# Smaller first loads, and x turned behind the products ahead of it, in a decoder-trunk step

## The chip, the cores and the metric

The kernel runs on one core of a Trainium2 chip. A core has TensorE (matrix products, PE in the profile, with PEld for its weight loads), VectorE (DVE), ScalarE (ACT), GpSimd (POOL) and SyncE (SP, which here issues most of the loads), and 16 DMA engines that move data between the chip's memory and the on-chip buffer. TensorE writes to PSUM, which the other engines read. Each engine works through its own instruction queue in order and waits on semaphores for the others.

The metric is the device time of one execution in microseconds (us); less is better. Where several executions were timed, the median is given.

## The reference

The reference computes one inference step of a decoder layer for 256 prompt tokens and 8 x 4 sample tokens, 288 tokens in all, with a model width of 2048, in float32:

```python
def rmsnorm(x, w):
    xf = x.astype(jnp.float32)
    y = xf * lax.rsqrt(jnp.mean(xf * xf, axis=-1, keepdims=True) + EPS)
    return (y * w.astype(jnp.float32)).astype(x.dtype)

def swiglu(x, w_in, w_out):
    gate, up = jnp.split(x @ w_in, 2, axis=-1)
    return (jax.nn.silu(gate) * up) @ w_out
...
        x = x + 0.5 * rmsnorm(swiglu(rmsnorm(x, g[0]), ffn1_w_in[l], ffn1_w_out[l]), g[1])
        m, sg, sh = hybrid_mixer(rmsnorm(x, g[2]), mix_w_in[l], gla_w_gate_up[l], gla_b_gate[l],
                                 gla_norm[l], lbs[l], hgrn_norm[l], mix_w_out[l], s_gla[l], s_hgrn[l])
        x = x + rmsnorm(m, g[3])
        x = x + 0.5 * rmsnorm(swiglu(rmsnorm(x, g[4]), ffn2_w_in[l], ffn2_w_out[l]), g[5])
```

There is one layer. The hidden width of each feed-forward part is 5632. The hybrid mixer runs two gated linear recurrences beside each other; the change does not touch it. The weights, some 365 MB, are read once.

## The kernel before

**Layout.** Activations lie turned: model width on the 128 partitions, tokens along the free axis. x is 16 tiles `x[k]` of 128 x 288 (256 prompt columns and 32 sample columns). Each product x @ w is taken with a weight tile of 128 x 128 as the stationary operand and a tile of 288 tokens as the moving one, and summed over the 16 values of k in PSUM.

**Three products for one.** Float32 operands are split into a high and a low part in the fast float32 format: `xh` and `xl` for activations (`split_to`, L241 to L244: ScalarE writes the high part, scaled by the norm's gain, and VectorE the low part), `wh` and `wl` for weights (`Weights.pieces`, L75 to L88: ScalarE copies, L86, and VectorE subtracts, L87). TensorE then takes `xh` with `wh`, `xl` with `wh`, and `xh` with `wl` (L464 to L466). The norm's per-token factor `rt` is not needed ahead of the products; it is multiplied in afterwards.

**Weights.** They come in units of 512 KB (two k rows of 512 columns) through `raw` buffers, of which there are three (`RAW_BUFS`). `load` (L55) issues one load on SyncE's queue; `fill` keeps three units loaded beyond the last one split; `ahead` splits units in advance, as many as the four `wh`/`wl` buffers hold. A `raw` buffer is free for the next load once its unit has been split.

**Blocks.** `block` (L455) runs the products of 512 output columns: for each unit of two k, four column groups f of three products, then a `tick(k)`, in which other work is put between products. The last unit runs column group by column group, and `evac` then moves the finished column group out of PSUM. The first two blocks of the kernel are `gate1_0` and `up1_0` in `ffn` (L499); in the first, `tick0` of `PreNorm` (L364) prepares a tile of x each k, and in the second, `tick1` sums the squares of x for the norm (`acc`, then `pre` and `rt` at k = 9). The gate tiles `g` are copied out of PSUM at L523 and get `rt` later.

**The start.** The norm gains go to `stage` over ScalarE's queue, are turned by TensorE (`tp_prm`, L269) and copied to `prm` (L270). x is loaded in four pieces of 512 columns (`xin`, L260 to L267), each as a prompt load of 512 KB and a sample load of 64 KB, with one weight unit behind each of the first three. `x_tile` (L272) turns one tile: three transposes into PSUM (L276, L277), a copy to `x[k]` by VectorE for even k (L281) and by ScalarE for odd k (L279), and the split into `xh` and `xl` from that copy. Four tiles are prepared ahead of the first product (`AHEAD`), with the first two units split in halves between them, each part pinned behind the one ahead of it (`issue_after`); the other twelve follow one for each `tick0`, four tiles ahead of use.

**Order.** A scheduler orders each engine's instructions by priority and estimated readiness; `issue_after` puts instructions behind a given one.

Of the kernel before, what the change touches and what calls it, by code (L numbers as in the profile page):

```python
# [23 lines left out]
KT = D // P  # L24
# [7 lines left out]
RAW_BUFS = 3  # L32
# [5 lines left out]
class Weights:  # L38
# [16 lines left out]
    def load(self):  # L55
        i, src = self.loaded, self.srcs[self.loaded]
        raw = self.rawp.tile([P, 1024], F32, name=f"raw{i}", tag="raw")
        if isinstance(src, list):
            for c, part in src:
                w = part.shape[2]  # L60
                self.nc.sync.dma_start(raw.rearrange("p (a b) -> p a b", b=512)[:, :, c:c + w], part)
        else:
            self.nc.sync.dma_start(raw.rearrange("p (a b) -> p a b", b=src.shape[2]), src)
        self.raws[i] = raw
        self.loaded += 1

    def fill(self):
        while self.loaded < min(len(self.srcs), self.split + RAW_BUFS):
# [2 lines left out]
    def part(self):  # L71
        for _ in self.pieces(1):
            pass
# [42 lines left out]
def trunk_kernel(ctx, tc, x_prompt, x_sample, state_gla, state_hgrn, norm_gains, f1_in, f1_out, f2_in, f2_out,  # L116
                 mix_in, gla_up, gla_b, gla_norm, hgrn_gamma, hgrn_norm, mix_out, masks,
                 y_prompt, y_sample, sgp, shp, sgs, shs):
    nc = tc.nc
    V, S, G, PE = nc.vector, nc.scalar, nc.gpsimd, nc.tensor  # L120
# [103 lines left out]
    lb = const.tile([P, 8], F32, name="lb")  # L224
    omlb = const.tile([P, 8], F32, name="omlb")

    AHEAD = 4
    UPDATED = 8
    EARLY = 4
# [8 lines left out]
    def gain(i, k):  # L238
        return prm[:, i * KT + k:i * KT + k + 1]

    def split_to(parts, src, col):  # L241
        i1 = S.activation(parts[0], src, AF.Copy, scale=col).ins
        i2 = V.scalar_tensor_tensor(parts[1], src, col, parts[0].bitcast(F32), op0=ALU.mult, op1=ALU.subtract).ins  # L243
# [6 lines left out]
    ldp = first.enter_context(tc.tile_pool(name="ld", bufs=4, side="right"))  # L250
# [6 lines left out]
    G.dma_start(stage2[12:14, :], gla_norm.rearrange("o (k p) -> (o k) p", p=P))  # L257
    G.dma_start(stage2[14:15, :], hgrn_norm)
    xins = []
    for s in range(4):  # L260
        xin = ldp.tile([P, 3, 512], F32, name=f"xin{s}", tag="xin")
        V.memset(xin[:, 2, :], 0.0)
        nc.sync.dma_start(xin[:, 0:2, :], x_prompt[0, :, s * 512:(s + 1) * 512].rearrange("(t p) c -> p t c", p=P))
        nc.sync.dma_start(xin[0:TS, 2, :], x_sample[:, :, s * 512:(s + 1) * 512].rearrange("b t c -> (b t) c"))
        xins.append(xin)
        if s < RAW_BUFS:
            W.load()  # L267
    tp = auxtile("tp_prm")
    PE.transpose(tp[:, 0:96], stage, ident[0:96, 0:96])  # L269
    V.tensor_copy(prm[:, 0:96], tp[:, 0:96])  # L270

    def x_tile(k):  # L272
        s, c = k // 4, slice(k % 4 * P, (k % 4 + 1) * P)
        tp = auxtile(f"tp_x{k}")
        for t in range(2):
            PE.transpose(tp[:, t * P:(t + 1) * P], xins[s][:, t, c], ident)  # L276
        PE.transpose(tp[:, TP:TP + P], xins[s][:, 2, c], ident)  # L277
        if k % 2:
            S.activation(x[k], tp[:, 0:T], AF.Copy)  # L279
        else:  # L280
            V.tensor_copy(x[k], tp[:, 0:T])  # L281
        return split_x(0, k)


    pin = ()
    for k in range(AHEAD):
        if k % 2 == 0:
            unit = W.pieces(2)
        for part in (lambda: x_tile(k), lambda: next(unit)):
            with ExitStack() as es:  # L290
                for i in pin:
                    es.enter_context(tc.issue_after(i))
                pin = part()
        if k % 2 == 1:
            W.fill()

    def prm2():
        tp = auxtile("tp_prm2")
        PE.transpose(tp[:, 0:P], stage2, ident)
        V.tensor_copy(prm[:, 96:111], tp[:, 0:15])  # L300


    V.tensor_scalar(hg1[:, 0:KT], prm[:, 16:32], 0.5, None, op0=ALU.mult)
    V.tensor_scalar(hg1[:, KT:], prm[:, 80:96], 0.5, None, op0=ALU.mult)

    def lower_bounds():

# [49 lines left out]
    class PreNorm:  # L357
# [4 lines left out]
            self.name, self.update, self.ahead, self.late = name, update, ahead, []  # L362

        def tick0(self, k):  # L364
            if k + self.ahead < KT:
                self.split = self.update(k + self.ahead)

        def tick1(self, k):
            if k < 8:
# [82 lines left out]
        return update  # L452


    def block(name, nk, rhs, evac, width=512, tick=None, tail=1, hold=False, most=99, fill=None):  # L455

        nf, per = width // P, 1024 // width
        nu = nk // per
        ps = [mmtile(f"{name}_{f}") for f in range(nf)]
        ws = [W.next() for _ in range(EARLY // per)] if fill else []  # L460

        def mm3(dst, w, f, k, parts, start, stop):
            c = (k % per) * width + f * P
            yield lambda: PE.matmul(dst, w[0][:, c:c + P], parts[0], start=start, stop=False)  # L464
            yield lambda: PE.matmul(dst, w[0][:, c:c + P], parts[1], start=False, stop=False)  # L465
            yield lambda: PE.matmul(dst, w[1][:, c:c + P], parts[0], start=False, stop=stop)  # L466

        def mm(w, f, k):
            if not fill or f or k >= EARLY:
                for ready in mm3(ps[f][:, 0:T], w, f, k, rhs(k), k == 0, k == nk - 1):  # L470
                    ready()

        if fill:
            fill.products(lambda dst, k, parts, stop: mm3(dst, ws[k // per], 0, k, parts, k == 0, stop), ps[0][:, 0:T])
        for u in range(nu - tail):
            w = ws.pop(0) if ws else W.next()
            for k in range(u * per, (u + 1) * per):
                for f in range(nf):
                    mm(w, f, k)
                if tick is not None:  # L480
                    tick(k)
            W.ahead(most)
            if fill and u == 5:
                fill.scaled()
        ws = [W.next() for _ in range(tail)]
        for f in range(nf):
            for k in range((nu - tail) * per, nk):
                mm(ws[k // per - (nu - tail)], f, k)
            evac(f, fill.total(ps[f][:, 0:T]) if fill and f == 0 else ps[f][:, 0:T])
        for k in range((nu - tail) * per, nk):  # L490
            if tick is not None:
                tick(k)
        if not hold:
            W.ahead()
# [4 lines left out]
    def ffn(tag, gcol, gnext, pn, before, fill=None):  # L499

        final = gnext is None
        border = []
        with ExitStack() as pools:
# [3 lines left out]
            def do_in(c):  # L507
                hh = fp.tile([P, 4, T], F32R, name=f"hh{tag}_{c}", tag="hh")
                hl = fp.tile([P, 4, T], F32R, name=f"hl{tag}_{c}", tag="hl")
                hid[c] = (hh, hl)  # L510
                gs = []

                def gate(g):
                    def run():
                        V.tensor_tensor(g, g, rt, op=ALU.mult)
                        act(g, g, AF.Silu)
                    return run

                def ev_gate(f, ps):
                    g = fp.tile([P, T], F32, name="g", tag="g", bufs=6)  # L520
                    gs.append(g)
                    if c == 0:
                        V.tensor_copy(g, ps)  # L523
# [752 lines left out]
```

## Time and profile before

| | |
|---|---|
| median of three runs | 2314.31 us (2312.02 to 2318.01) |
| the profiled execution, its own time | 2314.71 us |
| its span (first to last instruction) | 2312.9 us |
| TensorE busy | 2291.0 us, 99% of the span, 17352 matmul instructions |
| VectorE, ScalarE, GpSimd busy | 1421.2, 1012.7 and 64.4 us |
| read from and written to the chip's memory | 363.62 MB and 11.80 MB |

Numbers from a trace are of that one execution and count from its span's start. A matmul's duration overlaps that of the next, so the distance between two starts tells the pace. Busy time is an average over the whole span; where a change touches one stage only, the waits in that stage count.

### The profile page before, as it was taken

How to read it: one execution, taken by the hardware profiler on the slowest of the kernel's cores; microseconds unless marked ns; L12 is line 12 of the kernel's file. 1: busy time of each engine (PE TensorE's matmuls, PEld its weight loads, DVE VectorE, ACT ScalarE, POOL GpSimd, SP SyncE). 2: the span in 40 equal slices, each digit the busy share in tenths (PEclk: the TensorE clock that was granted, in tenths of full speed). 3: DMA queues.
4: the chain of work that ended last, by engine and by line, in shares of the span. 5: the costliest groups of instructions: out<-in, count | busy, mean ns of one | idle time of the engine just before them, and what ended most of it. 6: DMA issues, size and time to landing. Idle time of an engine off the chain costs nothing.

```text
span 2312.9 us, 42140 instructions
## 1 busy us (share of the span) xinstructions
PE 2291.0 (99%) x17352; PEld 2276.1 (98%) x17352; DVE 1421.2 (61%) x2314; ACT 1012.7 (44%) x1555; POOL 64.4 (3%) x110
## 2 busy tenths in 40 slices
PE   9999999999999999999999999999999999999998
PEld 8999999999999999999999999999999999999998
DVE  7545545554556568787889854854555555545545
ACT  6443333333334446454555554544333333333345
POOL 0000000000000001001001100100000000000000
PEclk9999999999999999999999999999999999999999
DMA  7555555555555545555555555455555555555553
GB/s 214 164 166 164 165 166 168 168 165 164 167 167 186 157 151 159 152 152 171 149 169 156 159 184 167 129 160 172 165 165 167 169 164 163 165 164 166 165 164 115
DMA packets 217008, 378.16 MB, mean 163 GB/s; under 512 B 15362, under 2 KB 52400, under 8 KB 216816
## 3 DMA queue, kind: packets, MB, share of 16 engines
q1 hardware_dynamic: 211264, 365.48, 52.6%
q0 software_dynamic: 3376, 9.81, 1.3%
q8 instruction: 136, 2.23, 0.4%
q10 hardware_dynamic: 2176, 0.18, 0.1%
q14 instruction: 56, 0.46, 0.1%
HBM read 363.62 MB, written 11.80 MB: 162 GB/s over the span
## 4 chain that ended last, share of the span: by engine, by line
PE 94%; DVE 3%; issue 1%; DMA 1%; ACT 1%; POOL 0%; DVEq 0%; SPq 0%; POOLq 0%; ACTq 0%
PE gate L465 9%; PE gate L466 9%; PE gate L464 9%; PE out L465 8%; PE out L466 8%; PE out L464 8%; PE up L466 8%; PE up L464 8%; PE up L465 8%; PE hfq L464 2%; PE hfq L465 1%; PE mo L466 1%; PE mo L464 1%; PE mo L465 1%; PE hfq L466 1%; PE sc L830 1%
## 5 line engine op out<-in xcount | busy, mean ns | idle before, releaser
L87 DVE TENSOR_TENSOR wl<-raw,wh 128x1024 fp32r<-128x1024 f32 (+1 forms) x674 | 821.1, 1219 | 629.1 <-ACT wh L86 626.5
L86 ACT ACTIVATE wh<-raw 128x1024 fp32r<-128x1024 f32 (+1 forms) x674 | 711.3, 1056 | 1073.3 <-PE gate L465 323.9
L465 PE MATMUL gate<-xl,wh 128*128 128x288 f32 x1660 | 489.2, 295 | 0.2 <-DVE xl L243 0.2
L464 PE MATMUL gate<-xh,wh 128*128 128x288 f32 x1660 | 488.4, 296 | 0.7 <-DVE z L1174 0.5
L466 PE MATMUL gate<-xh,wl 128*128 128x288 f32 x1660 | 488.7, 295 | 0.2 <-DVE wl L87 0.2
L465 PE MATMUL out<-hl,wh 128*128 128x288 f32 x1408 | 415.8, 295 | 0.0
L464 PE MATMUL out<-hh,wh 128*128 128x288 f32 x1408 | 415.6, 295 | 0.0
L466 PE MATMUL up<-xh,wl 128*128 128x288 f32 x1408 | 415.0, 295 | 0.0
L466 PE MATMUL out<-hh,wl 128*128 128x288 f32 x1408 | 415.0, 295 | 0.0
L464 PE MATMUL up<-xh,wh 128*128 128x288 f32 x1408 | 414.6, 294 | 0.3 <-DVE g L523 0.3
L465 PE MATMUL up<-xl,wh 128*128 128x288 f32 x1408 | 414.8, 295 | 0.0
L465 PEld LDWEIGHTS gate<-xl,wh 128*128 128x128 f32 x1660 | 311.7, 188 | 1.1 <-DVE xl L243 1.0
L464 PEld LDWEIGHTS gate<-xh,wh 128*128 128x128 f32 x1660 | 310.5, 188 | 1.6 <-DVE z L1174 0.7
L466 PEld LDWEIGHTS gate<-xh,wl 128*128 128x128 f32 x1660 | 311.4, 188 | 0.7 <-DVE wl L87 0.7
L466 PEld LDWEIGHTS out<-hh,wl 128*128 128x128 f32 x1408 | 264.7, 188 | 0.0
L464 PEld LDWEIGHTS up<-xh,wh 128*128 128x128 f32 x1408 | 264.1, 188 | 0.6 <-DVE g L523 0.5
L464 PEld LDWEIGHTS out<-hh,wh 128*128 128x128 f32 x1408 | 264.6, 188 | 0.0
L465 PEld LDWEIGHTS out<-hl,wh 128*128 128x128 f32 x1408 | 264.5, 188 | 0.0
L466 PEld LDWEIGHTS up<-xh,wl 128*128 128x128 f32 x1408 | 264.2, 188 | 0.1
L465 PEld LDWEIGHTS up<-xl,wh 128*128 128x128 f32 x1408 | 264.2, 188 | 0.1
L583 DVE TENSOR_TENSOR y<-out,y 128x288 f32<-128x288 f32 x288 | 121.4, 452 | 104.5 <-PE out L466 101.7
L464 PE MATMUL hfq<-xh,wh 128*128 128x288 f32 x256 | 78.7, 307 | 0.0
(342 smaller groups left out, 2581.6 us busy)
## 6 DMA issues: line engine op xcount, KB each, us to landing
raw<-in_ffn_w_in_dram SPq DMA_DIRECT2D x352, 512.0 KB, 3.6
raw<-in_ffn_w_out_dram SPq DMA_DIRECT2D x176, 512.0 KB, 3.7
raw<-in_mix_w_in_dram SPq DMA_DIRECT2D x64, 512.0 KB, 3.7
raw<-in_mix_w_in_dram SPq DMA_DIRECT2D x96, 256.0 KB, 3.3
raw<-in_mix_w_out_dram SPq DMA_DIRECT2D x32, 512.0 KB, 3.8
out_dram<-s POOLq DMA_DIRECT2D x32, 256.0 KB, 3.3
s<-in_state_gla_dram SPq DMA_DIRECT2D x16, 256.0 KB, 3.6
s<-in_state_hgrn_dram SPq DMA_DIRECT2D x16, 256.0 KB, 3.4
```

What stands on the lines that cost most here:

```text
L86: i1 = self.nc.scalar.activation(h[:, c], raw[:, c], AF.Copy).ins
L87: i2 = self.nc.vector.tensor_tensor(l[:, c], raw[:, c], h[:, c].bitcast(F32), op=ALU.subtract).ins
L464: yield lambda: PE.matmul(dst, w[0][:, c:c + P], parts[0], start=start, stop=False)
L465: yield lambda: PE.matmul(dst, w[0][:, c:c + P], parts[1], start=False, stop=False)
L466: yield lambda: PE.matmul(dst, w[1][:, c:c + P], parts[0], start=False, stop=stop)
L583: V.tensor_tensor(y[k], ps, y[k], op=ALU.add)
L830: PE.matmul(ps[0:m, c:c + 64], k[:, a, i * P:i * P + m], r, start=c == 0, stop=True, skip_group_check=True)
```

## The change

- x is loaded in eight pieces of 256 columns, and not in four of 512. Five are issued at the start, the others while the first block runs.
- The first weight unit is loaded as two rows of 256 KB (`load_row`). The order is: x piece 0, the two rows of unit 0, x piece 1, unit 1, x piece 2, unit 2, x pieces 3 and 4.
- `xh` and `xl` are split from the turned tile in PSUM; the copy to `x[k]` is put behind them.
- Two tiles of x, and not four, are turned ahead of the first product. Tile k + 2 is turned behind the last product of tile k (`product[0]`).
- Seven products of a constant tile stand ahead of the turning of the gains on TensorE, and three more ahead of the first product.
- Weight units beyond the first two are split one for each two tiles (`W.ahead(1)` in `x_first`), and no longer by the first block itself (`most=0`).
- The two small products for `hg1` go behind the first splits.

```diff
+    def load_row(self, k):
+        if k == 0:
+            self.raws[self.loaded] = self.rawp.tile([P, 1024], F32, name=f"raw{self.loaded}", tag="raw")
+        w = self.srcs[self.loaded].shape[2]
+        self.nc.sync.dma_start(self.raws[self.loaded][:, k * w:(k + 1) * w], self.srcs[self.loaded][:, k, :])
+        if (k + 1) * w == 1024:
+            self.loaded += 1
...
+    FIRST = 2
...
-    for s in range(4):
-        xin = ldp.tile([P, 3, 512], F32, name=f"xin{s}", tag="xin")
+    def load_x(j):
+        xin = ldp.tile([P, 3, TP], F32, name=f"xin{j}", tag="xin")
         V.memset(xin[:, 2, :], 0.0)
...
+    load_x(0)
+    W.load_row(0)
+    W.load_row(1)
+    load_x(1)
+    W.load()
+    load_x(2)
+    W.load()
+    load_x(3)
+    load_x(4)
+    def warm(n):
+        ps = auxtile("warm")
+        for _ in range(n):
+            PE.matmul(ps[:, 0:P], onesD, onesD, start=True, stop=True)
+
+    warm(7)
     tp = auxtile("tp_prm")
...
-        if k % 2:
-            S.activation(x[k], tp[:, 0:T], AF.Copy)
-        else:
-            V.tensor_copy(x[k], tp[:, 0:T])
-        return split_x(0, k)
+        ins = split_to((xh[k], xl[k]), tp[:, 0:T], gain(0, k))
+        with tc.issue_after(ins[0]), tc.issue_after(ins[1]):
+            if k % 2:
+                S.activation(x[k], tp[:, 0:T], AF.Copy)
+            else:
+                V.tensor_copy(x[k], tp[:, 0:T])
+        return ins
...
+    def x_first(k):
+        with tc.issue_after(product[0]) if k >= FIRST else ExitStack():
+            ins = x_tile(k)
+        if k < 4:
+            if k % 2 == 0:
+                unit.append(W.pieces(2))
+            with tc.issue_after(ins[0]), tc.issue_after(ins[1]):
+                ins = next(unit[-1])
         if k % 2 == 1:
+            if k >= 3:
+                with tc.issue_after(ins[0]), tc.issue_after(ins[1]):
+                    W.ahead(1)
             W.fill()
+            if k // 2 + 5 < KT // 2:
+                load_x(k // 2 + 5)
+        return ins
+
+    for k in range(FIRST):
+        ins = x_first(k)
+    warm(3)
...
-                    ready()
+                    product[0] = ready().ins
...
-                    block(f"gate{tag}_0", KT, xrhs, ev_gate, tick=pn.tick0, most=1 if final else 99, fill=fill)
+                    block(f"gate{tag}_0", KT, xrhs, ev_gate, tick=pn.tick0, most=1 if final else 0, fill=fill)
...
-    pn = PreNorm("pre1", x_tile, AHEAD)
+    pn = PreNorm("pre1", x_first, FIRST)
```

More of the change, by code (lines that the diff above doesn't have):

```diff
@@ L249, in trunk_kernel @@
     first = ExitStack()
-    ldp = first.enter_context(tc.tile_pool(name="ld", bufs=4, side="right"))
+    ldp = first.enter_context(tc.tile_pool(name="ld", bufs=8, side="right"))
     stage = ldp.tile([96, P], F32, name="stage", bufs=1)
@@ L259, in trunk_kernel @@
     xins = []
-    for s in range(4):
-        xin = ldp.tile([P, 3, 512], F32, name=f"xin{s}", tag="xin")
+    def load_x(j):
+        xin = ldp.tile([P, 3, TP], F32, name=f"xin{j}", tag="xin")
         V.memset(xin[:, 2, :], 0.0)
-        nc.sync.dma_start(xin[:, 0:2, :], x_prompt[0, :, s * 512:(s + 1) * 512].rearrange("(t p) c -> p t c", p=P))
-        nc.sync.dma_start(xin[0:TS, 2, :], x_sample[:, :, s * 512:(s + 1) * 512].rearrange("b t c -> (b t) c"))
+        c = slice(j * TP, (j + 1) * TP)
+        nc.sync.dma_start(xin[:, 0:2, :], x_prompt[0, :, c].rearrange("(t p) c -> p t c", p=P))
+        nc.sync.dma_start(xin[0:TS, 2, :], x_sample[:, :, c].rearrange("b t c -> (b t) c"))
         xins.append(xin)
-        if s < RAW_BUFS:
-            W.load()
+    load_x(0)
[12 more added lines that the diff above has]
+    warm(7)
     tp = auxtile("tp_prm")
@@ L272, in x_tile @@
     def x_tile(k):
-        s, c = k // 4, slice(k % 4 * P, (k % 4 + 1) * P)
+        xin, c = xins[k // 2], slice(k % 2 * P, (k % 2 + 1) * P)
         tp = auxtile(f"tp_x{k}")
         for t in range(2):
-            PE.transpose(tp[:, t * P:(t + 1) * P], xins[s][:, t, c], ident)
-        PE.transpose(tp[:, TP:TP + P], xins[s][:, 2, c], ident)
-        if k % 2:
-            S.activation(x[k], tp[:, 0:T], AF.Copy)
-        else:
-            V.tensor_copy(x[k], tp[:, 0:T])
-        return split_x(0, k)
[L285 to L293, printed above, removed]
+            PE.transpose(tp[:, t * P:(t + 1) * P], xin[:, t, c], ident)
+        PE.transpose(tp[:, TP:TP + P], xin[:, 2, c], ident)
+        ins = split_to((xh[k], xl[k]), tp[:, 0:T], gain(0, k))
[5 more added lines that the diff above has]
+        return ins
+    unit = []
+    def x_first(k):
[6 more added lines that the diff above has]
+                ins = next(unit[-1])
         if k % 2 == 1:
+            if k >= 3:
+                with tc.issue_after(ins[0]), tc.issue_after(ins[1]):
+                    W.ahead(1)
             W.fill()
+            if k // 2 + 5 < KT // 2:
[4 more added lines that the diff above has]
+    warm(3)
+    with tc.issue_after(ins[1]):
+        V.tensor_scalar(hg1[:, 0:KT], prm[:, 16:32], 0.5, None, op0=ALU.mult)
+        V.tensor_scalar(hg1[:, KT:], prm[:, 80:96], 0.5, None, op0=ALU.mult)
     def prm2():
@@ L300, in prm2 @@
         V.tensor_copy(prm[:, 96:111], tp[:, 0:15])
-    V.tensor_scalar(hg1[:, 0:KT], prm[:, 16:32], 0.5, None, op0=ALU.mult)
-    V.tensor_scalar(hg1[:, KT:], prm[:, 80:96], 0.5, None, op0=ALU.mult)
     def lower_bounds():
@@ L364, in tick0 @@
         def tick0(self, k):
-            if k + self.ahead < KT:
-                self.split = self.update(k + self.ahead)
+            for j in range(k + self.ahead, min(KT, k + self.ahead + 1)):
+                self.split = self.update(j)
         def tick1(self, k):
@@ L452, in post_norm @@
         return update
+    product = [None]
     def block(name, nk, rhs, evac, width=512, tick=None, tail=1, hold=False, most=99, fill=None):
```

## The prediction

> **What bounds the kernel.** I read the page's engine shares first, then the chain that ended last, and then the first 41 us in order of time, since the change ends there: on every engine the instructions stand in the order of before from the middle of the first up block on.
>
> ```profile
> PE 2291.0 (99%) x17352; PEld 2276.1 (98%) x17352; DVE 1421.2 (61%) x2314; ACT 1012.7 (44%) x1555; POOL 64.4 (3%) x110
> ...
> PEclk9999999999999999999999999999999999999999
> ...
> PE 94%; DVE 3%; issue 1%; DMA 1%; ACT 1%; POOL 0%; DVEq 0%; SPq 0%; POOLq 0%; ACTq 0%
> ...
> 300.00:400.00 100.00, 100.00 (x757) 100.00 (x756) 51.93 (x68) 37.37 (x44) 0.00 (x0) 1.00 0.55 165
> ```
>
> TensorE is busy for 2291.0 of 2312.9 us. The last row is a stretch in the middle of the feed-forward part, with busy us and count of each engine, then granted clock, DMA share and GB/s: TensorE starts 757 products in 100 us, one each 0.132 us, and never waits. So nothing can be won but the 21.9 us in which it is idle, and the change touches only the part of it that lies in the start. Rows in order of time give start, duration, engine, line, what is written and read, and in brackets the wait ahead of it:
>
> ```profile
> 4.73 0.40 PE L269 MATMUL tp_prm<-ident,stage 96*128 96x96 f32 x1 [4.73 <-DMA stage<-in_norm_gains_dram]
> 5.16 0.26 DVE L270 COPY prm<-tp_prm 128x96 f32<-128x96 f32 x1 [2.14 <-PE tp_prm L269]
> 5.19 0.29 PEld L276 LDWEIGHTS tp_x<-ident,xin 128*128 128x128 f32 x2 [0.31 <-DMA xin<-in_x_prompt_dram]
> ...
> 5.68 0.42 PE L277 MATMUL tp_x<-ident,xin 128*128 128x128 f32 x1
> ...
> 5.89 0.64 PE L276 MATMUL tp_x<-ident,xin 128*128 128x128 f32 x2
> ...
> 6.13 0.46 DVE L281 COPY x<-tp_x 128x288 f32<-128x288 f32 x1 [0.43 <-PE tp_x L277]
> ...
> 6.63 0.54 ACT L242 ACTIVATE xh<-x,prm 128x288 fp32r<-128x288 f32 x1 [4.11 <-DVE x L281]
> ...
> 7.20 0.52 DVE L243 SCALAR_TENSOR_TENSOR xl<-x,prm,xh 128x288 fp32r<-128x288 f32 x1 [0.60 <-ACT xh L242]
> ...
> 7.51 0.63 ACT L86 ACTIVATE wh<-raw 128x512 fp32r<-128x512 f32 x1 [0.35 <-DMA raw<-in_ffn_w_in_dram]
> ...
> 8.18 0.69 DVE L87 TENSOR_TENSOR wl<-raw,wh 128x512 fp32r<-128x512 f32 x1 [0.46 <-ACT wh L86]
> ...
> 8.93 0.40 PE L466 MATMUL gate<-xh,wl 128*128 128x288 f32 x1
> ```
>
> The gains land at 4.7 and reach `prm` at 5.42. x is turned, copied (6.13), split into `xh` (6.63) and `xl` (7.20); the weights are split once unit 0 has landed (7.51, 8.18). The first product with `wl`, the one from which TensorE runs on, starts at 8.93. After it TensorE stops four times:
>
> ```profile
> 10.10 0.30 PE L466 MATMUL gate<-xh,wl 128*128 128x288 f32 x1
> ...
> 10.70 0.29 PE L465 MATMUL gate<-xl,wh 128*128 128x288 f32 x1
> ...
> 12.61 0.29 PE L465 MATMUL gate<-xl,wh 128*128 128x288 f32 x1
> ...
> 13.16 0.30 PE L464 MATMUL gate<-xh,wh 128*128 128x288 f32 x1
> ...
> 16.74 0.29 PE L465 MATMUL gate<-xl,wh 128*128 128x288 f32 x1
> 17.20 0.40 PE L466 MATMUL gate<-xh,wl 128*128 128x288 f32 x1 [0.17 <-DVE wl L87]
> 17.43 0.29 PE L464 MATMUL gate<-xh,wh 128*128 128x288 f32 x1
> ...
> 35.97 0.29 PE L464 MATMUL gate<-xh,wh 128*128 128x288 f32 x1
> 36.50 0.40 PE L465 MATMUL gate<-xl,wh 128*128 128x288 f32 x1 [0.24 <-DVE xl L243]
> 36.73 0.30 PE L466 MATMUL gate<-xh,wl 128*128 128x288 f32 x1
> ...
> 39.93 0.29 PE L466 MATMUL up<-xh,wl 128*128 128x288 f32 x1
> 40.49 0.40 PE L464 MATMUL up<-xh,wh 128*128 128x288 f32 x1 [0.27 <-DVE g L523]
> 40.73 0.30 PE L465 MATMUL up<-xl,wh 128*128 128x288 f32 x1
> ```
>
> Two starts on take 0.26 us. Here they take 0.55, 0.69, 0.76 and 0.80 us, so the stops cost 0.28, 0.43, 0.50 and 0.53 us: 1.74 in all. The first pair of rows prices a turned tile: 0.60 us less two products is 0.34.
>
> **The change part by part.** *Loads.* What lands late now, and how fast bytes come, is in these rows (each number of the GB/s line is one us of the first 40; the rows with DMA as engine are steps of the chain, from issue to landing):
>
> ```profile
> GB/s 0 12 233 278 267 332 307 260 295 385 395 291 338 383 291 334 309 297 133 348 82 115 379 94 287 215 168 297 274 272 127 346 55 47 264 229 0 147 363 23
> ...
> 1.83 0.42 SPq L63 DMA_DIRECT2D raw<-in_ffn_w_in_dram  x1
> ...
> 1.83 5.66 DMA raw<-in_ffn_w_in_dram
> 10.28 7.46 DMA raw<-in_ffn_w_in_dram
> ...
> 17.77 1.06 ACT L86 ACTIVATE wh<-raw 128x1024 fp32r<-128x1024 f32 x1 [1.02 <-DMA raw<-in_ffn_w_in_dram]
> ...
> 1130.00:1180.00 50.00, 50.00 (x398) 48.93 (x396) 44.80 (x111) 23.41 (x53) 4.11 (x6) 1.00 0.54 157
> ```
>
> Unit 0 landed at 7.49, when 1.56 MB had come; it and all issued ahead of it are 1.16 MB. Unit 3 landed at 17.74 with 4.93 MB, and its own sum is 4.51. So a piece lands when its sum and 0.4 MB of later pieces have come. By that rule the changed order gives: first row of unit 0 (0.61 MB) 5.6 us, second row 6.5, unit 1 9.3, unit 2 11.4, unit 3 15.6. The shorter rows of x cost little: the mixer's loads of the same 1 KB rows (last row) move 157 GB/s at a share of 0.54, 291 at full share, against 165/0.55 = 300 for 2 KB rows. SyncE issues nine loads more at some 0.4 us each, 15 by about 9 us; unit 3 waits there for unit 0's buffer, which comes free at about 9, and only the last x loads stand behind it. The eight smaller memsets write the same elements as four did and lie in VectorE's wait before 5.16.
>
> The Trainium skill ("DMA: Bandwidth & Descriptors", Bandwidth) speaks against this part: about 2 us fixed for each DMA, so batch to 1 MiB and more. Paid one after the other, it would bring unit 0's first row only at about 8 us, an estimate from that page, and the start would be some 0.9 us later than now. Queued loads at 300 GB/s, where that fixed cost alone would give 163 GB/s for 512 KB, say that it overlaps.
>
> *The first product.* With x there by 4.8, the turn follows `tp_prm` at 4.9; its result is there at 5.8 at the pace of the rows at 5.68 and 5.89 (0.21 us each), 5.4 at half of that. `xh` reads it from PSUM, without the copy, once `prm` is there: start 5.47 to 5.80. From there VectorE's queue decides: `xh` 0.54, then `xl` (0.43 to the next start), the copy of x now behind it (0.38), `wl` 0.69, and 0.06 to the product, 2.1 to 2.15 us: 7.6 to 7.95, taken 7.8. Gain 1.1 us, ends 0.95 and 1.3. `wh` needs the first row at 5.9 to 6.25 (lands 5.6) and the second at 6.9 (6.5). The two small products for `hg1` go behind the splits, off the path. If reading PSUM costs `xl` or `xh` 0.1 us more, 0.2 of this goes.
>
> *The warming products.*
>
> ```profile
> 55.70 0.65 PE L353 MATMUL pre<-acc,onesD 128*128 128x288 f32 x2
> ...
> 56.18 0.27 PE L299 MATMUL tp_prm<-ident,stage 128*128 128x128 f32 x1
> ```
>
> A plain f32 product of 288 columns takes 0.48, so one of 128 takes 0.21, and 0.43 at the slow pace. Seven end by about 4.2, under the wait for the gains (4.73); without that cover they would cost up to 3 us. Three more stand between tile 1 and the first product, 0.6 to 1.3 us, ending at 6.2 to 7.5: under the wait for `wl`, at worst 0.2 on the path.
>
> *The shorter lead.* Tiles 0 to 3 were turned ahead of the products, now only 0 and 1: two more turns lie among the products, +0.67. Tile k+2 is turned behind product k, so `xh`, `xl` and the weights' split have one block of 1.92 us. For odd tiles `xl` is ready 1.4 us after the block ahead starts. The tight one is block 2: `xh`, `xl`, copy and `wl` in a row end some 0.1 us late, +0.15 (0 to 0.3). Later units: ScalarE takes unit 3 behind `xh` of tile 5, at about 16, and VectorE is done at 18.3, 1 us ahead of use. The last block has no such lead: its `xh` is there 0.85 us and its `xl` 1.4 after the block ahead starts, and TensorE has 0.66 us of other products before it: +0.3 (0.1 to 0.6).
>
> *Stops that go.* The first two came from units that landed late (now 2 us sooner). The third is `xl` behind a unit's split; the order of VectorE has it ahead. The fourth is the copy of gate tiles behind a split,
>
> ```profile
> 38.84 1.23 DVE L87 TENSOR_TENSOR wl<-raw,wh 128x1024 fp32r<-128x1024 f32 x1
> ```
>
> and the four copies now stand together ahead of the next split: all 1.74 go (at least the first two, 0.7). What is late next is the sum of squares, now behind these copies and seven products later on TensorE; it has slack: `rt` is done about 3 us ahead of the first up tile's use.
>
> *Sum:* -1.1 - 1.74 + 0.67 + 0.15 + 0.3 = -1.7 us (ends -0.4 and -2.4). From the profiled execution's 2314.71 us (span 2312.9 and 1.8 around it) that is 2313.0; it stood 0.4 above the median of 2314.31, so on the median **2312.6**.
>
> **The rivals.** *Loads come no sooner* because pieces share the engines: unit 0's first row then lands near 7.4 as the whole unit did. Start gain 0, the longer turns stay, half the stops go: 0.67 + 0.45 - 0.9 = +0.2, 2314.5. For it: ScalarE's waits for loads now; against: the landing rule above.
>
> *The pace comes late.* TensorE turned x at 0.21 us a transpose until 7.8 and ran products at full pace from 8.9 on, some 4.1 us after its first work, with the granted clock at 1.00 throughout. If the warming products do not count or the wait behind them sets the pace back, the first 3.4 to 4 us of products run at half pace: +1.7 to 2, and the time is 2314.4. The Trainium skill ("TensorE: Matmul & The Clock Gate", Part 1 and Part 4) states half clock until one window of about 3.4 us has been busy, and that transposes do not count as busy; the rows at 5.68 to 8.93 agree with the first and not with the second, as nearly all work before full pace was transposes.
>
> *Slower:* the lead of two makes ScalarE's queue the bound: `xh` of the next tile stands behind a unit whose load is late. Unit 3 has 0.35 us until ScalarE waits and 1 more until TensorE does. If units 3 to 9 came 2.5 us later than I work out, seven stops of 1.2 us follow: +8.4 - 1.7, 2321. The four stops of now happen with a lead of four, which speaks for it; that the queue in front of unit 3 is 0.6 MB shorter speaks against.
>
> *Nothing changes:* not likely at the start, but below what can be told: a difference of 0.3%, 7 us, is about what a measurement of this kernel can tell from none, as its three runs lie from 2312.02 to 2318.01.
>
> **How the numbers follow.** Forecast 0.60 (2312 to 2313.5), loads no sooner 0.15, pace late 0.15, small stops of the short lead that eat the gain (up to +5 us) 0.06, slower 0.02, and 0.02 for a gain beyond 7 us, which would need more than the 1.74 and the 8.9 us of the start hold between them. The first three and most of the fourth lie within 0.3%. The range takes in the ends of the sum, the two middle rivals and about 2 us of scatter of a median: 2309.8 to 2315.8. Chances: faster 0.02, same 0.95, slower 0.03.
>
> **What would show it.** In the changed trace: the first product with `wl` at 7.6 to 8.0; `tp_prm` still at 4.7, behind seven warming products done by 4.3; transposes of x at 0.11 us each; no stop of TensorE for a load from 12 to 18 us; one short stop in block 2 and one in the last gate block; the up block starting about 1.4 us sooner and without its stop. Wrong would be: `tp_prm` later than 5, products 0.24 us apart after 9 us, or ScalarE waiting for loads in each second block.

## The result and the profile after

Over 20 executions each, timed side by side, the changed kernel took 2310.52 us (median; 2309.52 to 2311.84) and the kernel before 2313.94 (2310.26 to 2318.01): ratio 0.9985, 95% interval 0.9978 to 0.9992. That is 3.4 us, 0.15%: far below the 2% from which a change counts as one here, though the interval lies clear of 1, and inside the range of the forecast, but twice the gain that the sum gave. The traces show that the gain is for the most part not the one that was summed: the start came out as forecast, most of it was given back 20 us later, and something else was gained in the mixer, which the change does not touch.

The profiled execution of the changed kernel took 2310.95 us, with a span of 2309.2. The engines' row of its page:

```profile
PE 2290.8 (99%) x17372; PEld 2276.7 (99%) x17372; DVE 1422.0 (62%) x2318; ACT 1012.1 (44%) x1555; POOL 64.2 (3%) x110
```

TensorE's busy time is nearly the same as before (2290.8 against 2291.0 us), but that hides two things: the ten warming products (20 instructions, 3.35 and 1.01 us) are new work in time that was idle, and in the mixer the kernel before spent some us at half clock, which lengthens its products. So the shares of busy and idle time do not tell where the 3.7 us of span went; the stages do.

*The start.* The changed kernel in order of time (start, duration, engine, line, what is written and read, and the wait ahead of it):

```profile
1.14 3.35 PE L294 MATMUL warm<-onesD 128*128 128x128 f32 x14 [1.14 <-POOL onesD L227]
4.28 0.37 PE L298 MATMUL tp_prm<-ident,stage 96*128 96x96 f32 x1
4.44 0.63 PE L305 MATMUL tp_x<-ident,xin 128*128 128x128 f32 x2
...
5.08 0.63 PE L305 MATMUL tp_x<-ident,xin 128*128 128x128 f32 x2
...
5.73 0.62 ACT L95 ACTIVATE wh<-raw 128x512 fp32r<-128x512 f32 x1
...
7.40 0.40 PE L510 MATMUL gate<-xh,wl 128*128 128x288 f32 x1 [0.40 <-DVE wl L96]
7.77 0.29 PE L509 MATMUL gate<-xl,wh 128*128 128x288 f32 x1
7.90 0.29 PE L510 MATMUL gate<-xh,wl 128*128 128x288 f32 x1
...
11.43 0.40 PE L510 MATMUL gate<-xh,wl 128*128 128x288 f32 x1
...
38.75 0.29 PE L508 MATMUL up<-xh,wh 128*128 128x288 f32 x1
```

The first product with `wl` starts at 7.40 and not at 8.93. From there products stand 0.13 us apart (7.77, 7.90), with a short stop in block 2 (the row at 11.43 takes 0.40 in place of 0.29), one of the same kind near 19.2 and one in the last gate block. The first product of the third `up` column group, behind the last of the old stops, starts at 38.75; before, it started at 40.49. That is 1.74 us sooner.

*Where this goes.* Here `pre`, the product that adds `acc` over the partitions, waits, in the changed kernel:

```profile
36.40 2.04 ACT L95 ACTIVATE wh<-raw 128x1024 fp32r<-128x1024 f32 x2
38.34 0.43 ACT L364 ACTIVATE acc<-x 128x288 f32<-128x288 f32 x1
...
43.78 1.06 ACT L95 ACTIVATE wh<-raw 128x1024 fp32r<-128x1024 f32 x1 [0.74 <-DMA raw<-in_ffn_w_in_dram]
...
54.45 2.14 DVE L368 TENSOR_TENSOR acc<-acc,sq 128x288 f32<-128x288 f32 x4
...
56.73 0.72 PE L395 MATMUL pre<-acc,onesD 128*128 128x288 f32 x2 [1.79 <-DVE acc L368]
```

The same in the kernel before, whose `pre` row at 55.70 stands in the prediction and has no wait:

```profile
35.52 0.43 ACT L322 ACTIVATE acc<-x 128x288 f32<-128x288 f32 x1
...
49.26 1.58 DVE L326 TENSOR_TENSOR acc<-acc,sq 128x288 f32<-128x288 f32 x3
```

Before, the sum of squares began at 35.52 and was done at 50.84, 4.9 us ahead of `pre`. Now it begins 2.8 us later, on ScalarE behind the split of two weight units (the row at 36.40), and on its way ScalarE, which splits the weights of the up block between the squares, waits four times for a weight load (0.74, 0.27, 0.64 and 0.89 us; before, none from 36 us on). The sum is done at 56.59, and TensorE stands still for 1.79 us. At the end of the first feed-forward part (the first `post` product; before, then after) nothing is left in this pair of profiles:

```profile
854.73 0.72 PE L333 MATMUL post<-onesD,acc 128*128 128x1 f32 x6
...
1447.13 0.72 PE L333 MATMUL postm<-onesD,acc 128*128 128x1 f32 x6
```

```profile
854.87 0.72 PE L375 MATMUL post<-onesD,acc 128*128 128x1 f32 x6
...
1442.62 0.72 PE L375 MATMUL postm<-onesD,acc 128*128 128x1 f32 x6
```

*Where the gain arises.* The second row of each, `postm`, is the end of the mixer. The mixer takes 592.40 us before and 587.75 after, though PE, DVE, ACT and POOL run it in the same order of instructions. The difference is 4.65 us, of which this execution loses 0.8 again by its end. It arises in two places. By the `hms` product near 998 us (before, then after) 1.17 us of it are there, counted from `post`:

```profile
998.77 0.40 PE L1009 MATMUL hms<-nh,ones 128*128 128x288 f32 x1 [0.54 <-ACT nh L1002]
...
997.74 0.40 PE L1053 MATMUL hms<-nh,ones 128*128 128x288 f32 x1 [0.54 <-ACT nh L1046]
```

Nearly all of the other 3.5 us lies around 1070 us. Before:

```profile
1071.02 0.45 PE L728 MATMUL tp_v<-ident,vt 128*96 128x128 f32 x1 [3.29 <-DVE vt L745]
...
1074.20 0.44 PE L465 MATMUL hfq<-xl,wh 128*128 128x288 f32 x1
...
1068.18 0.42 ACT L950 ACTIVATE hl<-s 128x256 fp32r<-128x256 f32 x1 [3.02 <-DMA s<-in_state_hgrn_dram]
1069.57 1.23 DVE L87 TENSOR_TENSOR wl<-raw,wh 128x1024 fp32r<-128x1024 f32 x1 [3.57 <-ACT wh L86]
1050.00:1100.00 50.00, 46.71 (x356) 45.77 (x355) 37.46 (x91) 19.87 (x49) 5.73 (x7) 0.93 0.51 151
```

After:

```profile
1065.78 0.42 ACT L994 ACTIVATE hl<-s 128x256 fp32r<-128x256 f32 x1 [0.73 <-DMA s<-in_state_hgrn_dram]
1067.17 1.23 DVE L96 TENSOR_TENSOR wl<-raw,wh 128x1024 fp32r<-128x1024 f32 x1 [2.16 <-ACT wh L95]
PE tp_v L772 <- DVE vt L789: 1.9, 1, 1.9
1050.00:1100.00 50.00, 47.81 (x383) 46.48 (x383) 39.80 (x96) 20.49 (x49) 5.41 (x7) 1.00 0.56 161
```

Read upwards, TensorE's turning of a v tile (`tp_v`) waits for `vt`; VectorE has `vt` behind `wl`; `wl` waits for ScalarE's `wh`; and that stands behind `hl`, which waits for the load of a recurrence state (`s`). That wait ended at 1068.18 before and at 1065.78 after, 2.4 us apart, of which 1.0 had arisen by 998 us. In the last rows (the stretch from 1050 to 1100 us: busy us and count of each engine, then the granted clock) the kernel before has a clock of 0.93 and 356 matmuls where the changed one has 1.00 and 383: behind its stop TensorE ran at half clock for a while, with longer products (the row at 1074.20: 0.44 in place of 0.29). The longer stop (3.29 against 1.9 us) and the half clock together cost it 27 matmuls in this stretch, about 3.6 us at 0.132 each.

### The profile page after: what moved, and what is told of

Its sections match the earlier page's. It is cut to its first block, busy times and chain, and to the rows that moved or that the text cites. A ratio compares the mean times of both kernels' runs of the same rounds, so it can differ in the third digit from the quotient of the medians.

```text
span 2309.2 us, 42203 instructions
## 1 busy us (share of the span) xinstructions
PE 2290.8 (99%) x17372; PEld 2276.7 (99%) x17372; DVE 1422.0 (62%) x2318; ACT 1012.1 (44%) x1555; POOL 64.2 (3%) x110
## 4 chain that ended last, share of the span: by engine, by line
PE 93%; DVE 4%; issue 1%; ACT 1%; DMA 1%; POOL 0%; DVEq 0%; ACTq 0%; POOLq 0%
PE gate L510 9%; PE gate L509 9%; PE gate L508 9%; PE out L509 8%; PE out L510 8%; PE out L508 8%; PE up L510 8%; PE up L509 8%; PE up L508 8%; PE hfq L508 1%; PE mo L510 1%; PE mo L508 1%; PE mo L509 1%; PE hfq L509 1%; PE hfq L510 1%; PE sc L874 1%
```

## The experiments

Each kernel ran beside the kernel before on the same chip. Where it is not said otherwise, before took 2314.56 us there (median); beside the runs without the writes and the last repeats of both kernels it took 2314.95.

**The kernel before, twice more.** No edit.

> The kernel before, unchanged, against itself. Theory A (the start wins 1.7 us, a stop of TensorE at the norm's sum, pre, gives it back, and the measured gain of 3.4 us arises in the mixer, where the profiled execution of before stopped 3.3 us for vt and then lost clock): ratio 1.000 within 0.0007; in its profile the first product with wl at 8.9 us, the first post product at 854.7 within 0.3, and again a stop for vt of about 3 us between 1050 and 1100 us with a granted clock under 1 there. Theory B (the first profile of before was an odd one in the mixer; the measured gain is the start's, kept to the end): the stop for vt is 2 us or less and the clock 1.00 there, and the span is 2310 to 2311.

> The kernel before, unchanged, for a further profile. Theory G (the mixer's stop varies from one execution to the next in this kernel, and its times spread over 8 us by it): a time near 2311 goes with a stop under 2.5 us and full clock, a time of 2313 or more with a stop of over 3 us and half clock behind it. Rival: the stop is 3.3 us at any time of the run.

Measured: 2313.26 us (2310.86 to 2316.05), ratio 0.9997 (0.9988 to 1.0005), for the first; one execution of 2312.72 for the second. The first's profile repeats the picture of before in the mixer: 592.06 us, stop 3.3 us, granted clock 0.97 from 1050 to 1100 us. Its `post` stands at 855.44, 0.4 later than expected at the latest. The second, its wait and then that stretch:

```profile
PE tp_v L728 <- DVE vt L745: 2.9, 1, 2.9
1050.00:1100.00 50.00, 46.80 (x374) 45.47 (x374) 40.11 (x95) 20.82 (x52) 5.55 (x7) 1.00 0.55 162
```

A stop of 2.9 us and no half clock: mixer 589.9 us. So the same kernel has mixers of 589.9 to 592.4 us, and both parts of the loss near 1070 us, the length of the stop and the half clock behind it, vary from one execution to the next. The part near 998 us does not: from `post` to `hms` it is 144.04, 144.33 and 143.95 us in the three profiles of this kernel. The time lies between the two cases that were expected, and so does the picture: a long stop, but full clock.

**The sum of squares two tiles later.** The changed kernel with

```diff
-            if k == 9:
+            if k == 11:
```

> The changed kernel with the sum of squares taken by TensorE at k = 11 of the up block, not at k = 9. Theory A: the stop of 1.8 us at pre goes, the first post product comes at 853.1 us (854.87 in the changed kernel), and if the mixer is as there the time falls by 1.7 us to about 2308.8. Rival: rt is then late for the up block's tiles, and the stop comes back there: post at 854.5 to 855, no gain.

Measured: 2308.48 us (2307.80 to 2309.66), ratio 0.9977 (0.9968 to 0.9986), 2.0 us below the changed kernel. Its `post`:

```profile
853.13 0.72 PE L375 MATMUL post<-onesD,acc 128*128 128x1 f32 x6
```

The waits of its first 60 us have none ahead of `pre`, and `post` is 1.74 us sooner than in the changed kernel. That this is to the hundredth what the up block had gained is luck, for in three profiles of the changed kernel's order (this one, its repeat and the run with seven loads more) the wait is 1.79, 1.00 and 0.79 us and `post` stands at 854.87, 854.21 and 853.78. But `post` less the wait is 853.0 to 853.2 in all three, where this run has it. This shows that the wait for the squares gives the start's gain back, all of it in the first profile and about half in the others. The mixer of this run took 587.7 us, as in the changed kernel.

**No warming products.** The changed kernel with

```diff
-    warm(7)
+    warm(0)
...
-    warm(3)
+    warm(0)
```

> The changed kernel without the ten warming products. Theory A: the slow pace then reaches into the first block and the up block starts 0.3 to 0.8 us later, but the stop at pre, whose sum does not wait for TensorE, is shorter by as much: post at 854.9 within 0.2, time that of the changed kernel within 1 us. Rival (the pace counts): post later by 0.4 to 1.7 us. By the sentence of the Trainium skill (TensorE: Matmul & The Clock Gate, Part 4) that transposes do not count as busy, products would stay at half pace for 3.4 us after the first of them, 1.7 us.

and the same edit on the run with the sum of squares two tiles later:

> The sum of squares taken up two tiles later, as in the run before with that edit, and now without the ten warming products. Theory E (the warming products bring the full clock 2 to 4 us sooner, which the wait for the sum of squares hid in the run without them): the products between 7.6 and about 10 us run at half pace, the first `post` product comes 1 to 1.5 us later than with them (853.1), about 854.3, time 2309.6 us. Rival (they are worth nothing): `post` at 853.1, time 2308.5 us.

Measured: 2310.15 us (2309.43 to 2313.06) and 2307.42 (2306.90 to 2310.36; ratio 0.9972, 0.9962 to 0.9982). Without them the products run at the slow pace for longer; the first of these two kernels:

```profile
4.15 0.39 PE L298 MATMUL tp_prm<-ident,stage 96*128 96x96 f32 x1 [4.15 <-DMA stage<-in_norm_gains_dram]
...
8.49 0.44 PE L510 MATMUL gate<-xh,wl 128*128 128x288 f32 x1
...
10.49 0.30 PE L510 MATMUL gate<-xh,wl 128*128 128x288 f32 x1
```

Full pace came near 10.4 us here and near 8.7 in the second kernel; in the traces' records of the granted clock full clock begins at 10.37 and 8.68, and with the warming products at 6.09 (the changed kernel) and 5.79 (the sum two tiles later). The first product starts at 6.41 and 6.37 in the two cold kernels, so full pace came 4.0 and 2.3 us behind it; half pace for 3.4 us from the first product, as in the first expectation's last sentence, did not hold in the second. So the warming products bring the full pace 3 to 4 us sooner and are worth nothing to the time. In the first run the wait for the squares takes it back, as expected: that wait is 0.83 us and `post` is at 854.93. In the second, where the wait is gone, the expected loss of 1 to 1.5 us did not come either: `post` stands at 853.23, 0.1 us behind that of the run with the warming products. Why is open. The second run was even 1.1 us (0.4 to 1.6) below its like with the warming products, which ran on another chip; as its `post` is not sooner, that lies behind it (0.7 us in the mixer, 587.0 us). It is the fastest complete kernel of the study.

**Four tiles ahead.** The changed kernel with

```diff
-    FIRST = 2
+    FIRST = 4
```

> The changed kernel with four tiles of x turned ahead of the products, and a lead of four, as before the change. Theory A: the first product with wl comes 0.3 to 1 us later, the squares of x are done earlier, the stop at pre falls from 1.8 to under 0.5 us, and post comes at 853.5 to 854.3. Rival (the squares are late for another cause, the units' loads or the order of the splits): the stop stays over 1 us and post at 854.9 or later.

Measured: 2312.25 us (2310.99 to 2314.17), ratio 0.9993 (0.9985 to 1.0002), 1.7 us above the changed kernel. Two waits of its profile, and its first `pre`:

```profile
PE tp_v L772 <- DVE vt L789: 2.5, 1, 2.5
PE tp_x L305 <- DVE xl L253: 2.0, 1, 2.0
...
55.16 0.65 PE L395 MATMUL pre<-acc,onesD 128*128 128x288 f32 x2
```

TensorE stands 2.0 us at the start, since the third turned tile needs a PSUM buffer that the first's split has yet to release, and the first product with `wl` comes at 8.85, later than expected. In exchange the wait for the squares is gone (the row of `pre`, near 55 us): with this lead ScalarE takes the first square at 35.67, as in the kernel before, waits for no load in the up block, and the sum is done at 53.07. So the squares are late by the lead of two and the later splits and loads that go with it. `post` is at 854.20, within the range of the changed kernel's own profiles, so the longer lead wins nothing that can be told at the start. The mixer of this profile, one of the quicker executions (2311.15 us), took 588.8 us, with a stop of 2.5; where the median's 1.7 us arise, it does not show.

**Nine loads more, seven loads more.** Into `load` of the kernel before went the first two lines, and into that of the changed kernel the last two:

```diff
+        if 60 <= i < 69:
+            self.nc.sync.dma_start(raw[0:1, 0:8], src[0:1, 0, 0:8])
...
+        if 60 <= i < 67:
+            self.nc.sync.dma_start(raw[0:1, 0:8], src[0:1, 0, 0:8])
```

> The kernel before with nine extra loads of 32 bytes in the first feed-forward part (32 bytes of weight units 60 to 68 are loaded a second time), as many loads as the change adds on SyncE's queue; every other engine's order is that of before. Theory C (the place of the state loads in the rotation of loads decides how they land in the mixer, and so the 3.3 us stop ahead of the turned v tiles and the half clock behind it): the mixer behaves as in the changed kernel, stop of 1 to 2.5 us, granted clock 1.00 from 1050 to 1100 us, 587 to 589 us from the first `post` product to the first `postm` product, time 2311 us. Theory D (the number of loads ahead of it has no part in it): stop of 3.3 us, clock under 1.00, 592 us, time 2314 us.

> The changed kernel with seven extra loads of 32 bytes in the first feed-forward part, so that the number of loads ahead of the mixer is that of before plus sixteen. Theory C: the mixer falls back to that of before, stop of 3.3 us, half clock behind it, 592 us, time 2313.5 us. Theory D: 587 to 589 us, time 2310.5 us, as the changed kernel.

Measured: 2312.94 us (2311.18 to 2316.17), ratio 0.9996 (0.9987 to 1.0004), and 2310.75 (2309.47 to 2313.32), ratio 0.9987 (0.9979 to 0.9996). The times stay with the kernel that each was made from, as the theory without the count has it. The profiled execution of the first, however, is one of its quick ones, 2311.47 us:

```profile
PE tp_v L730 <- DVE vt L747: 1.6, 1, 1.6
1050.00:1100.00 50.00, 48.09 (x385) 46.76 (x385) 40.91 (x97) 21.16 (x52) 5.62 (x7) 1.00 0.55 163
```

The order of before with a stop of 1.6 us, full clock, and a mixer of 588.7. Again the stop and the half clock, by which the two kernels differ, differ also between executions of one order. From `post` to `hms`, however, this run takes 144.01 us as the kernel before does, and the other, with the changed kernel's order, 142.77.

**The new sample states not written.** In both kernels the write of the new sample states is left out, so that this output is missing:

```diff
-                    G.dma_start(ss_out[b0:b0 + nb, a].rearrange("b p v -> p b v"), s)
+                    if b0 < 0:
+                        pass
```

> The kernel before without the write of the new sample states to memory (it is left out, so this part of the output is missing); the state loads of the mixer then wait for no write-out, and nothing else shares the transfer engines with them. The planner orders the mixer somewhat differently for it. Theory F (the mixer's stops and the half clock behind them come from state loads that wait for and share with these writes): stop ahead of the turned v tiles under 1 us, granted clock 1.00 from 1050 to 1100 us, under 587 us from the first `post` to the first `postm` product, runs within 2 us of each other but for the start, median near 2309. Rival (they come from the weight loads alone): stop and spread as before, 2314 us.

> The same write left out of the changed kernel. Theory F: the mixer is that of the run without the writes on the kernel before, so the difference of the two is what the start leaves, which the wait for the sum of squares gives back: within 0.8 us of it. Rival (the change gains by something behind the start that is not the mixer's state loads): still about 3.4 us below it.

Measured: 2308.67 us (2307.31 to 2310.83) for the kernel before and 2307.96 (2306.92 to 2309.32) for the changed one. Of the 3.4 us between the two, 0.7 are left, and with 9 and 8 executions that lie over each other these cannot be told from none. The 9 executions of before spread over 3.5 us, not over the 2 that were expected; 16 of the complete kernel beside them spread over 4.7, so a smaller spread is not shown. From 1050 to 1100 us, the kernel before without the writes, then the changed one:

```profile
1050.00:1100.00 50.00, 49.69 (x397) 48.40 (x396) 41.75 (x101) 22.39 (x53) 2.07 (x3) 1.00 0.49 132
```

```profile
1050.00:1100.00 50.00, 49.68 (x399) 48.49 (x398) 41.00 (x99) 22.26 (x54) 2.81 (x3) 1.00 0.50 136
```

The stop at `tp_v` is gone in both, and the mixers take 585.5 and 586.0 us. The state loads normally wait on SyncE until a write-out has left their buffer; here, before and then after, are SyncE's waits from 1040 to 1075 us in the complete kernels:

```profile
SPq L787 <- DMA out_dram<-s: 21.5, 7, 6.3
```

```profile
SPq L831 <- DMA out_dram<-s: 15.6, 6, 3.9
```

The sum of these waits is 20.7 to 22.8 us in all four complete profiles of before's order (the run with nine loads more is one of them) and 12.9 to 19.1 in all seven of the changed one (with the runs that edit its start). So the kernels differ in state loads that wait for write-outs, and without the write-outs the difference is gone; whether the loads lose more by the wait or by sharing the transfer engines is not told apart. The expectation holds but for the spread, with one reserve: the scheduler orders the mixer differently once the writes are out, so the two runs tell where the difference hangs, but not what the writes cost by themselves.

**The changed kernel once more.** No edit.

> The changed kernel, unchanged, for a second profile. Theory G: stop of 1 to 2.5 us in the mixer, full clock behind it, 2309.5 to 2311.8 us; the wait for the sum of squares near 57 us is there again, 0.5 to 2 us.

Measured: 2310.94 us, with the wait at `pre` at 1.0 us and `post` at 854.21. In the mixer (waits; then stretches of TensorE with busy us, count, granted clock, DMA share and GB/s):

```profile
PE tp_v L772 <- DVE vt L789: 2.2, 1, 2.2
1069.25:1069.50 0.25, 0.25 (x3) 0.50 0.41 115
...
1072.50:1072.75 0.25, 0.25 (x3) 0.87 0.89 90
```

The stop lies in the expected range, but half clock follows it, which was not expected: for about 3.4 us, from 1069.1 to 1072.6. The mixer took 589.1 us, so the changed kernel is not free of this either; to the `hms` product, though, it took 142.83 us, as in the changed kernel's first profile (142.87).

## Why the prediction was right or wrong

The forecast of 2312.6 us lay 2.1 us above the median, within its range. That no large change would come was right; that less than some 7 us could not be told from none was not, for with 20 executions of each kernel side by side the 3.4 us are clear of none. That the time fell in the range is in part luck, as most of the gain came from where the prediction did not look. By its steps:

- *What bounds it:* right in the main: TensorE stays the bound. But "nothing can be won but the 21.9 us in which it is idle" left out its pace, which half clock lowered near 1070 us, and "the change touches only the part of it that lies in the start" was too narrow: the stop of 3.3 us at `tp_v` was the largest behind the start, and it moved.
- *Loads and first product:* right in mechanism, small in size. The first product with `wl` was put at 7.8 (7.6 to 7.95) and came at 7.40: 1.53 us gained against 1.1. The cause is the landing of the gains, taken as fixed at 4.7. They land by 4.28 (4.15 in the run without warming products). The first row of unit 0 came in time for `wh` at 5.73; the second kept `wh` waiting for 0.32 us, until 7.06, where 6.5 was forecast, off the path of the first product. The Trainium skill's rule that would have spoken against this part ("DMA: Bandwidth & Descriptors", Bandwidth: batch transfers to 1 MiB and more) does not show here: the first row was there by 5.73, where the estimate from that page was about 8.
- *Warming products:* the seven took 3.35 us, half a microsecond each, so they ended at 4.49 and not at 4.2, and the transposes behind them kept the slow pace of 0.21 us (4.44, 4.87, 5.08) where 0.11 was expected. From the second product (6.71) on the pace was full. The rival that the pace comes late was wrong about this kernel, and wrong about the price as well: the run without them lost nothing. Its "granted clock at 1.00 throughout" is no reading for the start: the trace's record of the clock begins with full clock, at 8.71 us in the kernel before, and the view counts what lies ahead of it as 1.00.
- *Shorter lead and stops:* right in the main. Short stops where the two were forecast and one more near 19.2, none of TensorE's for a load; all four old stops gone.
- *The start's sum:* -1.7 us forecast, -1.74 measured at the third `up` column. That they agree so closely is luck: 1.53 of it was won by the first product (1.1 forecast), and only 0.21 behind it (1.74 - 0.67 - 0.15 - 0.3 = 0.62 forecast).
- *What is late next:* this step failed. It named the right thing, the sum of squares behind the four copies, and dismissed it with "it has slack: `rt` is done about 3 us ahead of the first up tile's use". That is the slack of `rt`, not of TensorE: `pre` stands in TensorE's own queue, and whatever is behind it waits too. The slack that counted was 4.9 us between the end of `acc` and `pre`; the later start took 2.8 of it, and the longer way from the first square to the last (18.25 us against 15.32) took 2.9 more, with 2.5 us on it in which ScalarE waited for weight loads. ScalarE waiting for loads is a sign that the prediction had named as one of being wrong; it came in the up block. Moving `pre` down the order by seven products gave 0.9 back, and the up block that starts sooner took 1.7: 4.9 - 5.7 + 0.9 - 1.7 leaves 1.6 us too little, and the wait was 1.79.
- *The mixer:* not in the prediction at all. Its rivals all lay in the start. Of the 3.4 us some 2.7 hang on the state loads in the mixer and the write-outs, as far as the runs without the writes tell. The profiles agree: in four of before's order (with the run of nine loads more) `post` stands at 855.0 and the mixer takes 590.8 us in the mean, in three of the changed one 854.3 and 588.2, so that about 0.7 us is kept from the start and 2.6 won in the mixer, an estimate from few executions.

What stays open is why the state loads land later in the order of before. From `post` to `hms` the four profiles of that order take 143.95 to 144.33 us and seven of the changed one 142.77 to 143.25, so about 1 us of the mixer's gain goes with the kernel and not with the execution. The stop near 1070 us varies: it was 3.3, 3.3, 2.9 and 1.6 us in the four and 1.9, 2.2, 2.0, 1.1 and 2.5 in five of the new order, and 1.7 and 1.1 in the two runs with the sum of squares later, whose mixer is ordered a little differently in its first part. The mixer begins within 2.4 us of the same time in all of them, and the number of loads ahead of it is not the cause. A cause by when the loads meet the write-outs would fit; it was not shown.

## What to carry to other kernels

When work is moved earlier on the bounding engine, look for the next instruction in that engine's own queue that waits for another engine, and compute the slack there, not at the point where its result is used; moving that one instruction a little later can be worth as much as the change itself (2.0 us here, by one number). When executions of one kernel spread over more than a change is expected to bring, find in two profiles where the spread arises before reading a difference of medians as an effect of the edit. A stop on the bounding engine may cost more than its length, so the price of the stop includes the pace of what follows it.

## What the hardware showed that was not expected

A stop of TensorE in the middle of the kernel can halve its clock. The kernel before, around its stop of 3.29 us that ends at 1071.02 (stretches of TensorE, columns as above):

```profile
1070.25:1070.50 0.25, 0.00 (x0) 0.52 0.06 16
...
1077.00:1077.25 0.25, 0.25 (x3) 0.83 1.08 381
```

The clock is down to 0.52 from 1070.25 on and back to full within 1077.00 to 1077.25, after about 6.8 us, in 6.1 of which TensorE had work. The third profile of this kernel, with a stop of 2.9 us and full clock, shows the price: its mixer is 2.5 us shorter, 0.4 of it by the shorter stop, so the half clock cost about 2.1 us. In the second profile of this kernel a stop of 3.3 us, and in the second of the changed kernel one of 2.2 us, is followed by about 3.4 us at half clock. So the length of the stop alone does not decide it.

The Trainium skill ("TensorE: Matmul & The Clock Gate", Part 1) states that the clock is halved after an idle window of some 3.4 us, and that these windows run free of the kernel. The lengths of about 6.8 and 3.4 us agree with windows of that size. A whole window of idleness is not needed, though: in all three cases TensorE was idle for less than 3.4 us.

The traces let the windows be laid out. Their records of the granted clock have lengths of 6.827 and 3.413 us at half clock, and the time at full clock ahead of each drop is a multiple of 3.413 (1061.545 us, 311 of them, in the kernel before). Counted on in this step from the first full clock of each trace, the stop of the three profiles that lost clock puts 2.5, 3.2 and 2.2 us of idleness into one window, and the clock drops at that window's end. In the eight other complete profiles the stop puts at most 1.74 us into any window; the stop of 2.9 us falls on a boundary, 1.55 us ahead of it and 1.32 behind. The most that passed elsewhere is 1.96 us, at the start of the run with four tiles ahead. So among full products 2.2 us of idleness in a window of 3.41 were enough and 1.96 were not, and the place of a stop in the windows decides as much as its length. Idle time is not the whole measure, though: at the kernel's end the clock also falls behind windows that look busy (3.22 of 3.41 us in the changed kernel, from 2296.44 on) but hold turned tiles and products of one column.
